# Seven block products for the second half of w_ff2, and S5's input shuffled in whole rows

## The chip, the core and the metric

One core of a Trainium2 chip runs the whole program. Its engines work side by side, each through its own list in order: TensorE (PE, matmuls; its weight loads are shown as PEld), VectorE (DVE), ScalarE (ACT), GpSimd (POOL) and SyncE (SP, which only issues transfers here). The metric is device time in microseconds (us), lower is better.

## The reference

One layer of a decoder trunk on 1024 tokens of width 1024. What the change touches is the feed-forward network at its end and the input of one of three mixers, S5:

```python
proj = h @ w_in[l]
aq, ak, av, su, cq, ck, cv, cg = jnp.split(proj, offsets, axis=-1)
o_b = s5_mixer(su, ...)     # 16 groups x 16 channels, 64 complex states a group
...
x = x + ga1 * (mix @ w_out[l])
h = rms_norm(x, norm2_g[l]) * (1 + sc2) + sh2
x = x + ga2 * (jnp.square(jax.nn.relu(h @ w_ff1[l])) @ w_ff2[l])
```

w_ff1 is 1024 x 4096, w_ff2 4096 x 1024. `ga2` is one row of 1024 gates, the same for all tokens.

## The kernel before

Every float32 product is made of three matmuls (`mm3`, line 369): each operand is split into a high part (an ACT copy that rounds) and a low part (a difference on DVE or POOL), and high x high, high x low and low x high are added up in PSUM. So a weight page of 128 x 1024 costs one load, one ACT copy and one difference before PE can use it.

The feed-forward network runs in two halves of 512 tokens. The hidden width is cut into 32 blocks of 128 (`NF`). `ff1` makes one block for 512 tokens: 8 x 3 matmuls of 512 columns into one PSUM bank, then relu, square and the split (`ff_act`). `ff2` takes two blocks and one half of the output width: for each of four tiles of 128 tokens 2 x 3 matmuls of 512 columns, which DVE adds into the accumulator `z[n]`. After the last pair DVE multiplies `z[n]` by the gates (`rows_of[5]`), adds the residual `x2[n]`, and SP stores the tile. The second half begins when all tokens are normed (`N2 7`), some 1080 us into the program, and nothing but the feed-forward network is left then. `load_ff` loads a weight page, copies the high part on ACT and takes the low part on POOL.

S5 (`s5`, line 1003) gets its input `su` in four PSUM banks, channel by partition. ACT and DVE copy them into two pages `ut`, by position within a chunk of eight tokens; SP writes these to a scratch tensor in HBM, `su_d`, and reads them back with another layout into two pages `Ur`. `build` makes S5's weights, splits them and splits `Ur` (tiles named k); `apply` multiplies.

The order is not that of the code: all calls are recorded with a rank, a list scheduler (`arrange`, line 173) plays them through with its own prices, and the program is issued in the order that comes out. It also hands out the SBUF pages: 38 pages of 1024 floats per partition (`b`), 10 of 804 (`u`), 4 of 1088 (`k`) and a few others (`SLOTS`). All issued instructions therefore carry one line, that of the replay (2002 before, 2201 after). PSUM has eight banks, printed pa0 to pa3 (`sg`) and pb0 to pb3 (`sh`).

Of the kernel before, what the change touches and what calls it, by code (L numbers as in the profile page):

```python
# [9 lines left out]
F32 = mybir.dt.float32  # L10
# [3 lines left out]
ALU = mybir.AluOpType  # L14
# [6 lines left out]
NT = 8  # L21
# [289 lines left out]
def trunk(ctx: ExitStack, tc: tile.TileContext, I, out):  # L311
# [686 lines left out]
                tt(r, r, dd[:, g2 * 8 + hf * 4:g2 * 8 + hf * 4 + 4], ALU.add)  # L998
        yield 0

    su_d = dr.tile([2, 2, 65536], F32, name="su_d")

    def s5():

        for g2 in range(2):
            ut = page(1024)
            utv = ut.rearrange("f (j c) -> f j c", j=8)
            for q in range(2):
                src = sh[g2 * 2 + q].rearrange("f (c j) -> f j c", j=8)
                d = utv[:, :, q * 64:q * 64 + 64]  # L1010
                if q == 0:
                    A.activation(out=d, in_=src, func=AF.Copy)
                else:
                    V.tensor_copy(out=d, in_=src)
            nc.sync.dma_start(out=su_d[:, g2].rearrange("hf (q c) -> hf q c", q=64), in_=ut)
        done.add("s5 taken")
        Ur = [page(1024) for _ in range(2)]
        for hf in range(2):
            for j in range(8):
                nc.sync.dma_start(  # L1020
                    out=Ur[hf][j * 16:j * 16 + 16].rearrange("p (g c) -> p g c", g=8),
                    in_=su_d[hf].rearrange("g2 (g p j c) -> j p (g2 g) c", g=4, p=16, j=8)[j])
        W, Us = [], []
        Y = [page(1024) for _ in range(2)]
        Sj = [page(1024) for _ in range(2)]
# [884 lines left out]
        spawn(T + 9, late_proj())  # L1910


    z, f_of, w_of = {}, {}, {}
    pace, ahead = [X_FF], [X_AHEAD]

    def load_ff(unit):
# [29 lines left out]
    def ff2(half, p, dh, b):  # L1946
# [3 lines left out]
            load_row(5)  # L1950
        for t in range(4):
            n = half * 4 + t
            if n not in z:
                z[n] = page(1024)
            if last and not dh:
                x2[n] = page(1024)
                nc.sync.dma_start(out=x2[n], in_=x2_d[n])
            o, s, d = take("f2"), t * 128, z[n][:, c]
            for e in range(2):
                f = f_of[half, p * 2 + e]  # L1960
                w = slice(e * 512, e * 512 + 512)
                mm3(o, f[:, s:s + 128], f[:, 512 + s:640 + s], b[0][:, w], b[1][:, w], e == 0, e == 1)
            if p == 0:
                V.tensor_copy(out=d, in_=o)
            else:
                tt(d, o, d, ALU.add)
            if last:
                tt(d, d, rows_of[5][:, c], ALU.mult)
                tt(d, d, x2[n][:, c], ALU.add)
                if dh:  # L1970
                    nc.sync.dma_start(out=out[n * 128:n * 128 + 128, :], in_=z[n])
            yield 1.28 * pace[0]

    def feed_forward():
        units, h = [], NF // 2
        for q in range(NF + 1):
            for e in range(2):
                if q < NF:
                    units.append((1, q // h, q % h * 2 + e, 0))
                if q:  # L1980
                    units.append((2, (q - 1) // h, (q - 1) % h, e))
        loaded = 0
        for j, u in enumerate(units):
# [2 lines left out]
                loaded += 1  # L1986
            kind, half, i, dh = u
            if kind == 1:
                if half:
                    while f"N2 {NT - 1}" not in done:  # L1990
                        yield 1.0
                    pace[0] = 1.0
                yield from ff1(half, i, w_of.pop(u))
            else:
                yield from ff2(half, i, dh, w_of.pop(u))

    run_plan()
    order, span, start, end = arrange(calls, tag_of, SLOTS)
# [8 lines left out]
def pack(inputs):  # L2007
# [21 lines left out]
    wog = lambda a: a.reshape(2, 3, 64, 1024).transpose(1, 0, 2, 3).reshape(3, 128, 1024)  # L2029
    wi = I["w_in"][0]  # L2030
    span = lambda *ab: np.concatenate([np.arange(a, b) for a, b in ab])
    cols = [span((640, 896)), span((0, 384)), span((384, 640)), span((896, 1280), (2048, 2066)),
            span((1280, 1408), (1664, 1792)), span((1408, 1664)), span((1792, 2048))]
    group = lambda a: a.reshape(4, 2, 128, -1).transpose(0, 2, 1, 3).reshape(-1)
    return dict(
# [29 lines left out]
```

## Time and profile before

| | |
|---|---|
| three runs | 1436.9, 1441.61 (median), 1446.45 us |
| profiled execution | 1440.49 us, its span 1438.8 us |
| busy, share of the span | PE 93%, DVE 57%, ACT 53%, POOL 53% |
| granted TensorE clock, mean | 0.965 of 2.4 GHz |
| matmuls | 7218 recorded |
| DMA | 160.5 MB, 112 GB/s in the mean |

The page gives sums over one execution. A tile's name is that of the program without its number. "Idle before" is the time for which an engine stood still ahead of an instruction, and the name behind the arrow is what ended it. A timeline merges instructions of one kind that follow each other, and shows those waits in brackets. The chain of waits is followed back from the last instruction to what released it.

### The profile page before, as it was taken

To read this page: it belongs to the slowest core of one execution; us is meant where nothing else is said; L and a number is where in the kernel's file an instruction comes from. 1 tells how busy PE (TensorE), PEld (TensorE's weight loads), DVE (VectorE), ACT (ScalarE), POOL (GpSimd) and SP (SyncE) were. 2 spreads that over 40 slices of the span, in tenths; PEclk is the share of its full clock that TensorE was granted. 3 is DMA by queue.
4 is the path that set the end of the run, shared out by engine and by line. 5 is a ranking of instruction groups with operands and counts; after the bars stand their busy time and mean duration, and the time that the engine had idled before them with its cause. 6 is when DMAs were issued, how large, how long until landed. Compare 5 with 4: busy or idle time off the path is not lost.

```text
span 1438.8 us, 20631 instructions
## 1 busy us (share of the span) xinstructions
PE 1343.4 (93%) x7218; PEld 1154.1 (80%) x7218; DVE 813.2 (57%) x1846; ACT 760.8 (53%) x1774; POOL 759.8 (53%) x700
## 2 busy tenths in 40 slices
PE   5796799899899868999999999999999999999997
PEld 4696799899798646888888888888888888888886
DVE  7863777688688764556466565464538222222225
ACT  5265548667779766655565565552263333233331
POOL 2654683512556544546555555675557655554650
PEclk9888999999999887999999999999999999999999
DMA  9415334531315231222222222233444332233231
GB/s 357 141 51 163 128 101 159 176 100 58 111 42 177 90 123 46 94 67 70 74 79 87 79 96 74 79 127 138 160 176 175 104 108 97 89 104 101 88 118 58
DMA packets 58185, 160.54 MB, mean 112 GB/s; under 512 B 6468, under 2 KB 22370, under 8 KB 58082
## 3 DMA queue, kind: packets, MB, share of 16 engines
q1 hardware_dynamic: 50273, 145.33, 30.3%
q10 hardware_dynamic: 7808, 13.91, 2.6%
q8 instruction: 56, 0.92, 0.3%
q14 instruction: 48, 0.39, 0.1%
HBM read 140.07 MB, written 19.14 MB: 111 GB/s over the span
## 4 chain that ended last, share of the span: by engine, by line
PE 77%; DVE 6%; ACT 5%; DMA 1%; issue 1%; POOL 0%; ACTq 0%; SPq 0%; POOLq 0%; DVEq 0%
PE pb L2002 43%; PE pa L2002 33%; DVE b L2002 3%; ACT b L2002 3%; ACT u L2002 1%; DVE pb L2002 1%; DMA cq_d<-s 1%; DVE u L2002 1%; DVE k L2002 0%; DMA b<-in_ada_dram 0%; DVE s L2002 0%; DVE small L2002 0%; ACT s L2002 0%; POOL s L2002 0%; ACT k L2002 0%
## 5 line engine op out<-in xcount | busy, mean ns | idle before, releaser
L2002 PE MATMUL pb<-b,b 128*128 128x512 f32 (+2 forms) x2646 | 634.4, 386 | 3.6 <-DVE b L2002 2.4
L2002 PEld LDWEIGHTS pb<-b,b 128*128 128x128 f32 (+1 forms) x2646 | 478.4, 190 | 93.7 <-DVE b L2002 3.1
L2002 POOL TENSOR_TENSOR b<-b,b 128x1024 fp32r<-128x1024 f32 (+6 forms) x172 | 388.9, 2274 | 107.5 <-ACT b L2002 83.2
L2002 PE MATMUL pa<-b,b 128*128 128x256 f32 (+3 forms) x1890 | 352.4, 334 | 11.1 <-ACT s L2002 6.7
L2002 PEld LDWEIGHTS pa<-b,b 128*128 128x128 f32 (+1 forms) x1890 | 286.4, 195 | 41.0 <-ACT s L2002 7.0
L2002 DVE TENSOR_TENSOR b<-pa,b 128x512 f32<-128x512 f32 (+3 forms) x158 | 98.3, 622 | 245.7 <-PE pa L2002 242.8
L2002 ACT ACTIVATE b<-b 128x1024 fp32r<-128x1024 f32 (+2 forms) x195 | 187.9, 983 | 66.9 <-DVE b L2002 39.8
L2002 PE MATMUL pa<-u,b 128*128 128x384 f32 (+2 forms) x836 | 206.5, 366 | 5.6 <-ACT u L2002 2.6
L2002 POOL TENSOR_TENSOR b<-r,b 128x512 fp32r<-128x512 f32 x65 | 85.6, 1316 | 174.5 <-ACT b L2002 174.4
L2002 ACT ACTIVATE r<-pb 128x512 f32<-128x512 f32 x64 | 38.2, 597 | 244.8 <-PE pb L2002 244.8
L2002 PEld LDWEIGHTS pa<-u,b 128*128 128x128 f32 x836 | 147.8, 206 | 16.3 <-ACT u L2002 7.7
L2002 ACT ACTIVATE u<-pa 128x384 fp32r<-128x384 f32 (+4 forms) x205 | 97.1, 479 | 93.4 <-PE pa L2002 90.9
L2002 DVE TENSOR_TENSOR b<-pb,b 128x512 f32<-128x512 f32 (+2 forms) x150 | 98.1, 657 | 71.2 <-PE pb L2002 66.9
L2002 DVE TENSOR_TENSOR u<-pa,u 128x384 fp32r<-128x384 f32 (+1 forms) x173 | 95.0, 553 | 63.3 <-ACT u L2002 60.0
L2002 POOL TENSOR_SCALAR u<-u,small 128x256 f32<-128x256 f32 (+3 forms) x90 | 52.7, 596 | 115.8 <-DVE small L2002 77.7
L2002 POOL TENSOR_SCALAR b<-b,small 128x64 f32<-128x64 f32 (+8 forms) x118 | 78.2, 672 | 59.9 <-DVE small L2002 50.6
L2002 PE MATMUL pa<-wide,b 128*128 128x128 f32 (+1 forms) x443 | 83.9, 301 | 16.2 <-DVE b L2002 10.3
L2002 ACT ACTIVATE b<-b,small 128x128 f32<-128x128 f32 x256 | 93.3, 524 | 5.5 <-DMA b<-in_ada_dram 3.3
L2002 PEld LDWEIGHTS pa<-wide,b 128*128 128x128 f32 (+1 forms) x443 | 58.8, 151 | 35.1 <-DVE b L2002 13.0
L2002 DVE TENSOR_TENSOR b<-b,b 128x512 f32<-128x512 f32 (+3 forms) x78 | 78.2, 1028 | 11.1 <-ACT b L2002 5.3
L2002 PE MATMUL pb<-k,u 128*128 128x320 f32 (+10 forms) x300 | 71.3, 344 | 10.1 <-ACT u L2002 6.2
L2002 ACT ACTIVATE b<-pb,small 128x64 f32<-128x64 f32 (+4 forms) x130 | 62.5, 494 | 28.8 <-DVE small L2002 25.7
(148 smaller groups left out, 1492.6 us busy)
## 6 DMA issues: line engine op xcount, KB each, us to landing
b<-in_ff_dram SPq DMA_DIRECT2D x128, 512.0 KB, 3.8
b<-in_ada_dram SPq DMA_DIRECT2D x48, 512.0 KB, 4.6
b<-in_x_dram SPq DMA_DIRECT2D x16, 512.0 KB, 9.5
b<-in_wo_dram SPq DMA_DIRECT2D x16, 512.0 KB, 4.5
r<-in_w_in_dram SPq DMA_DIRECT2D x16, 256.0 KB, 2.8
b<-in_cw_dram SPq DMA_DIRECT2D x8, 512.0 KB, 5.0
x_d<-b ACTq DMA_DIRECT2D x8, 512.0 KB, 3.4
b<-x_d SPq DMA_DIRECT2D x8, 512.0 KB, 5.6
```

Source lines behind the costliest of these rows:

```text
L2002: method(*args, **kw)
```

## The change

**S5's input.** The scratch tensor gets the shape [2, 8, 128, 128]. A page `ut` is written with its 128 partitions outermost, each in eight runs of 128 floats, instead of two halves of 64 rows of 1024 floats. `Ur` is read in four transfers of 128 rows of 512 floats instead of sixteen of 16 x 8 x 128. The columns of `w_in` for `su` are put in another order on the host, so that position and channel stand where whole rows need them.

On SP, where the stored input of S5 leaves and comes back (b_196 and b_197 are the pages `ut`, b_198 and b_199 the pages `Ur`), before:

```order
L2002 DMA b138_219<-in_ada_dram 128x1024
L2002 DMA su_d_98<-b115_196 2x64x1024
L2002 DMA su_d_98<-b116_197 2x64x1024
L2002 DMA b117_198<-su_d_98 16x8x128 x8
L2002 DMA b118_199<-su_d_98 16x8x128 x8
L2002 DMA b147_228<-in_ada_dram 128x1024
```

and now:

```order
L2201 DMA b138_219<-in_ada_dram 128x1024
L2201 DMA su_d_98<-b115_196 128x8x128
L2201 DMA su_d_98<-b116_197 128x8x128
L2201 DMA b117_198<-su_d_98 128x512
L2201 DMA b118_199<-su_d_98 128x512
L2201 DMA b117_198<-su_d_98 128x512
L2201 DMA b118_199<-su_d_98 128x512
L2201 DMA b147_228<-in_ada_dram 128x1024
```

The place in the queue is the same; the shapes changed, and sixteen reads became four, of which the first two read what the first write stored.

On ACT, at the same stage (k127 and k143 are the high parts of the two pages `Ur`, b123 and b124 S5's weights out of PSUM, b146 belongs to the conditioning, s129 and u130 to a projection), before:

```order
L2002 ACTIVATE b146_227<-b138_219,small_71 128x128 x2
L2002 ACTIVATE s129_210<-pa1_64 128x384
L2002 ACTIVATE u130_211<-pa1_64 128x384
L2002 ACTIVATE b123_204<-pb1_68 128x4x64
L2002 ACTIVATE b124_205<-pb1_68 128x4x64
L2002 ACTIVATE k127_208<-b117_198 128x1024
L2002 ACTIVATE b146_227<-b138_219,small_71 128x128 x4
L2002 ACTIVATE k143_224<-b118_199 128x1024
```

and now:

```order
L2201 ACTIVATE b137_218<-b114_195,small_71 128x128 x5
L2201 ACTIVATE k127_208<-b117_198 128x1024
L2201 ACTIVATE k143_224<-b118_199 128x1024
L2201 ACTIVATE b123_204<-pb1_68 128x4x64
L2201 ACTIVATE b124_205<-pb1_68 128x4x64
L2201 ACTIVATE b123_204<-pb3_70 128x4x64
L2201 ACTIVATE b124_205<-pb3_70 128x4x64
L2201 ACTIVATE b123_204<-pb0_67 128x4x64
L2201 ACTIVATE b124_205<-pb0_67 128x4x64
L2201 ACTIVATE b146_227<-b138_219,small_71 128x128 x2
L2201 ACTIVATE s129_210<-pa1_64 128x384
L2201 ACTIVATE u130_211<-pa1_64 128x384
```

Both copies of `Ur` moved ahead of all eight evacuations of the weights (the last two follow these rows) and of two of the projection's.

**Second half of w_ff2.** Of its 16 pairs of hidden blocks the first 14 are taken in seven groups of four blocks (`NG` = 7). A group is a product of 512 tokens x 512 hidden x 1024 outputs, cut in two along each side, so of eight block products; it is now made of seven, with sums of blocks formed beforehand and afterwards (Strassen's scheme in Winograd's form). Sums of weight blocks (`right`) and of activation blocks (`left_rest`) are formed on DVE, split into high and low, and each product (two tiles of 128 tokens, 2 x 3 matmuls of 512 columns each) is added by DVE into one or two of six accumulators. The last group's four blocks are multiplied as before (`last_ff2`), with the gates multiplied into its weights (`load_last`); the seven groups' accumulators get their sums, the gates and the residual in `finish_block`, so that `last_ff2` adds and stores, half a tile at a time.

```diff
-    su_d = dr.tile([2, 2, 65536], F32, name="su_d")
+    su_d = dr.tile([2, 8, 128, 128], F32, name="su_d")
...
-            nc.sync.dma_start(out=su_d[:, g2].rearrange("hf (q c) -> hf q c", q=64), in_=ut)
+            nc.sync.dma_start(out=su_d[g2].rearrange("j f c -> f j c"), in_=utv)
...
-            for j in range(8):
-                nc.sync.dma_start(
-                    out=Ur[hf][j * 16:j * 16 + 16].rearrange("p (g c) -> p g c", g=8),
-                    in_=su_d[hf].rearrange("g2 (g p j c) -> j p (g2 g) c", g=4, p=16, j=8)[j])
+            for g2 in range(2):
+                src = su_d[g2].rearrange("j (p hf g) c -> hf (j p) (g c)", p=16, hf=2)[hf]
+                nc.sync.dma_start(out=Ur[hf][:, g2 * 512:g2 * 512 + 512], in_=src)
...
-                if dh:
-                    nc.sync.dma_start(out=out[n * 128:n * 128 + 128, :], in_=z[n])
+                nc.sync.dma_start(out=out[n * 128:n * 128 + 128, c], in_=d)
...
+    PRODUCTS = {1: ("X", ("C11", "U")), 2: ("Y", ("C11",)), 6: ("Z", ("U",)), 7: ("X", ("P7",)), 5: ("Y", ("P5",)),
+                4: ("Z", ("P4",)), 3: ("X", ("P3",))}
...
+    def split_right(g, m, x):
+        hi, lo = page(1024), page(1024)
+        copy_hi(hi, x)
+        split_lo(V, lo, x, hi)
+        right_of[g, m] = hi, lo
+    def right(g, m):
+        B = wraw[g]
+        if m == 1:
+            B["T1"] = page(1024)
+            tt(B["T1"], B[0, 1], B[0, 0], ALU.subtract)
+        elif m == 2:
+            B["T2"], B["T4"] = page(1024), page(1024)
+            tt(B["T2"], B[1, 1], B["T1"], ALU.subtract)
+            tt(B["T4"], B[1, 0], B["T2"], ALU.subtract)
+        elif m == 6:
+            tt(B[0, 1], B[1, 1], B[0, 1], ALU.subtract)
+        split_right(g, m, B[{1: (0, 0), 2: (1, 0), 6: "T2", 7: (0, 1), 5: "T1", 4: "T4", 3: (1, 1)}[m]])
...
+    def split_left(g, m, src):
+        left_of[g, m] = u = page(1024)
+        two = lambda x: x.rearrange("p (e t) -> p e t", e=2)
+        copy_hi(two(u[:, 0:512]), src)
+        split_lo(V, two(u[:, 512:1024]), src, two(u[:, 0:512]))
...
+        split_left(g, 2, a(0, 1))
+        s1 = of(a(1, 0), a(1, 1), ALU.add)
+        s2 = of(s1, a(0, 0), ALU.subtract)
+        split_left(g, 6, s2)
+        yield
+        split_left(g, 7, of(a(0, 0), a(1, 0), ALU.subtract))
+        split_left(g, 5, s1)
+        yield
+        split_left(g, 4, a(1, 1))
+        split_left(g, 3, of(a(0, 1), s2, ALU.subtract))
...
+    def product(g, m):
+        bank_, to = PRODUCTS[m]
+        b, u = right_of.pop((g, m)), left_of.pop((g, m))
+        for s in range(2):
+            o = dict(X=sg[2:4], Y=sg[0:2], Z=sh[2:4])[bank_][s]
+            for e in range(2):
+                l = e * 256 + s * 128
+                w = slice(e * 512, e * 512 + 512)
+                mm3(o, u[:, l:l + 128], u[:, 512 + l:640 + l], b[0][:, w], b[1][:, w], e == 0, e == 1)
+            for name in to:
...
+                    tt(d, o, d, ALU.add)
...
+    def finish_block(m, dh, d):
+        if d == "P5":
+            acc["U5"] = page(1024)
+            tt(acc["U5"], acc["U"], acc["P5"], ALU.add)
+            tt(acc[d], acc["U5"], acc["P7"], ALU.add)
+        else:
+            for x in {"P4": ("P7", "U"), "P3": ("U5",)}.get(d, ()):
+                tt(acc[d], acc[d], acc[x], ALU.add)
+        for s in range(2):
+            n, c = 4 + m * 2 + s, slice(dh * 512, dh * 512 + 512)
+            z_at[n, dh] = o = acc[d][:, s * 512:s * 512 + 512]
+            tt(o, o, rows_of[5][:, c], ALU.mult)
+            tt(o, o, x2[n][:, c], ALU.add)
...
+        tt(two(raw), two(raw), row.to_broadcast([128, 2, 512]), ALU.mult)
...
+    def last_ff2():
...
+                tt(d, o, d, ALU.add)
+                nc.sync.dma_start(out=out[(4 + t) * 128:(5 + t) * 128, c], in_=d)
...
+        for g in range(NG):
+            after = [[("p", g, m) for m in ms] for ms in ((1, 2), (6, 7), (5, 4), (3,))]
+            for e in range(4):
+                f = [("f", g * 4 + 4 + e)]
+                items += after[e] + f if g == NG - 1 and e == 3 else f + after[e]
```

The last lines set the order: a block of w_ff1 for the next group, then products 1 and 2; a block, 6 and 7; a block, 5 and 4; a block, 3.

On DVE, in the middle of the second half, before (accumulators b1292 to b1295, banks pa and pb):

```order
L2002 TENSOR_TENSOR b1292_1373<-pa3_66,b1292_1373 128x512
L2002 TENSOR_TENSOR b1293_1374<-pb2_69,b1293_1374 128x512
L2002 TENSOR_TENSOR b1294_1375<-pb3_70,b1294_1375 128x512
L2002 TENSOR_TENSOR b1295_1376<-pa2_65,b1295_1376 128x512
L2002 TENSOR_TENSOR b1292_1373<-pa3_66,b1292_1373 128x512
```

and now, around product 3 of a group (b1365 is accumulator P3, b1414 and b1430 the next group's activations, u1446, u1447 and u1453 sums of their blocks, b1445, b1448, b1451 to b1454 left blocks; b1319 and b1320 are the accumulators C11 and U of product 1):

```order
L2201 TENSOR_TENSOR b1365_1446<-pa2_65,b1365_1446 128x512
L2201 TENSOR_TENSOR u1446_1527<-b1414_1495,b1430_1511 128x512
L2201 TENSOR_TENSOR b1445_1526<-b1430_1511,b1445_1526 128x512
L2201 TENSOR_TENSOR u1447_1528<-u1446_1527,b1414_1495 128x512
L2201 TENSOR_TENSOR b1451_1532<-u1446_1527,b1451_1532 128x512
L2201 TENSOR_TENSOR b1452_1533<-b1430_1511,b1452_1533 128x512
L2201 TENSOR_TENSOR b1448_1529<-u1447_1528,b1448_1529 128x512
L2201 TENSOR_TENSOR u1453_1534<-b1430_1511,u1447_1528 128x512
L2201 TENSOR_TENSOR b1365_1446<-pa3_66,b1365_1446 128x512
L2201 TENSOR_TENSOR b1454_1535<-u1453_1534,b1454_1535 128x512
L2201 TENSOR_TENSOR b1319_1400<-pa2_65,b1319_1400 128x512
L2201 TENSOR_TENSOR b1320_1401<-pa2_65,b1320_1401 128x512
```

Before, DVE had only one addition per PSUM bank in this half; now seven operations between SBUF tiles stand between the two evacuations of one product, and an eighth ahead of product 1's.

## Rows read from the trace of the kernel before

**Rows 1.** The page: busy us of the engines; the chain by engine.

```profile
PE 1343.4 (93%) x7218; PEld 1154.1 (80%) x7218; DVE 813.2 (57%) x1846; ACT 760.8 (53%) x1774; POOL 759.8 (53%) x700
...
PE 77%; DVE 6%; ACT 5%; DMA 1%; issue 1%; POOL 0%; ACTq 0%; SPq 0%; POOLq 0%; DVEq 0%
```

**Rows 2.** Busy time of each engine (and instructions) in stretches of 100 us.

```profile
core 0: us, PE busy (x) PEld busy (x) DVE busy (x) ACT busy (x) POOL busy (x), PEclk, DMA share, GB/s
...
100.00:200.00 100.00, 76.44 (x506) 74.11 (x506) 56.97 (x91) 52.88 (x141) 59.47 (x50) 0.89 0.43 133
...
1100.00:1200.00 100.00, 100.00 (x443) 82.82 (x442) 29.67 (x43) 37.10 (x50) 58.83 (x30) 1.00 0.41 142
1200.00:1300.00 100.00, 100.00 (x443) 82.84 (x442) 26.13 (x38) 33.81 (x45) 58.31 (x29) 1.00 0.30 98
1300.00:1400.00 100.00, 100.00 (x443) 82.84 (x442) 25.03 (x37) 33.84 (x45) 54.13 (x27) 1.00 0.32 106
```

**Rows 3.** The chain of waits near the end: start, us, what.

```profile
1408.21 5.44 PE pb L2002 x24
```

**Rows 4.** Timeline of SP's queue: start us, us, what.

```profile
91.18 1.22 SPq L2002 DMA_DIRECT2D su_d<-b  x2
114.26 7.72 SPq L2002 DMA_DIRECT2D b<-su_d  x16
```

**Rows 5.** Waits of SP's queue: in total, times, longest.

```profile
SPq L2002 <- DMA su_d<-b: 21.7, 1, 21.7
```

**Rows 6.** Timeline of all engines: start us, us, what [idle before].

```profile
105.31 0.67 ACT L2002 ACTIVATE b<-pb 128x256 fp32r<-128x256 f32 x2
...
120.72 1.06 ACT L2002 ACTIVATE k<-b 128x1024 fp32r<-128x1024 f32 x1 [14.74 <-DMA b<-su_d]
...
121.80 1.23 DVE L2002 TENSOR_TENSOR k<-b,k 128x1024 fp32r<-128x1024 f32 x1 [15.04 <-ACT k L2002]
...
121.83 0.79 PE L2002 MATMUL pb<-b,k 128*128 128x256 f32 x2 [14.31 <-ACT k L2002]
```

**Rows 7.** Two short stretches, columns as in group 2.

```profile
100.00:105.00 5.00, 5.00 (x31) 4.93 (x31) 2.27 (x7) 3.64 (x12) 0.00 (x0) 0.81 0.13 52
...
115.00:117.00 2.00, 0.00 (x0) 0.00 (x0) 0.00 (x0) 0.00 (x0) 0.00 (x0) 0.50 0.42 124
```

**Rows 8.** DMA queues, and issues with size and median us to landing.

```profile
q10 hardware_dynamic: 7808, 13.91, 2.6%
...
b<-in_ff_dram SPq DMA_DIRECT2D x128, 512.0 KB, 3.8
...
r<-in_w_in_dram SPq DMA_DIRECT2D x16, 256.0 KB, 2.8
...
out_dram<-b SPq DMA_DIRECT2D x8, 512.0 KB, 3.2
```

**Rows 9.** Groups by shape, 1060 to 1430 us: busy us, mean ns.

```profile
L2002 POOL TENSOR_TENSOR b<-b,b 128x1024 fp32r<-128x1024 f32 x67 | 161.7, 2438 | 12.4 <-ACT b L2002 12.4
...
L2002 ACT ACTIVATE b<-b 128x1024 fp32r<-128x1024 f32 x63 | 63.0, 1044 | 8.6 <-DMA b<-in_ff_dram 8.6
...
L2002 DVE TENSOR_TENSOR b<-b,b 128x512 f32<-128x512 f32 x26 | 26.9, 1078 | 0.1
L2002 ACT ACTIVATE r<-r 128x512 f32<-128x512 f32 x33 | 20.9, 632 | 1.0
```

**Rows 10.** Timeline: DVE near 129 us, PE and DVE at the end.

```profile
128.82 1.22 DVE L2002 TENSOR_TENSOR k<-b,k 128x1024 fp32r<-128x1024 f32 x1
129.95 1.21 DVE L2002 TENSOR_REDUCE s<-b 128x128 f32<-128x1024 f32 x1
...
1428.45 1.52 PE L2002 MATMUL pa<-b,b 128*128 128x512 f32 x6
...
1432.67 0.68 DVE L2002 TENSOR_TENSOR b<-pa,b 128x512 f32<-128x512 f32 x1
1433.27 2.01 DVE L2002 TENSOR_TENSOR b<-b,b 128x512 f32<-128x512 f32 x3
```

## What the change will do to the time: the prediction

> **What bounds the kernel now.** I read the page first: TensorE (PE) is busy for 93% of the span and holds 77% of the chain that ended last [rows 1]. Then the table by stretches of 100 us: the share is not even. From 1100 to 1400 us PE is busy for every microsecond at full clock, while DVE, ACT and POOL stand at a quarter, a third and a half; between 100 and 200 us it is busy for only three quarters [rows 2]. So there are two different places. In the second half of the feed-forward network matmuls are the bound: only fewer of them shorten it. The chain prints 24 of them in 5.44 us, back to back [rows 3], 0.2267 us each. In the early place something else is waited for.
>
> The timelines around 91 to 122 us show what. SP issues the two writes of S5's input at 91.18 and then nothing until 114.26; of this, 21.7 us are put down to the landing of those writes [rows 4, 5]. Behind it PE idles 14.3, ACT 14.7 and DVE 15.0 us, all three ending with the copy of the shuffled input at 120.72 [rows 6]: the whole core stands still. In the middle of the write the DMA share is 0.13, two of sixteen engines, at 52 GB/s [rows 7]; two is also the outermost dimension of the write.
>
> **S5's shuffle.** Removed: the 2x64x1024 writes and sixteen reads of 64 KB, issued over 7.72 us [rows 4]. Added: two writes whose outermost dimension is 128 partitions, in 512 B runs (1024 per write), and four reads of 256 KB in 2 KB runs. No row shows this write. Its bounds: reads in 512 B runs moved 124 GB/s at a share of 0.42 [rows 7], so 0.42 x 16 x 2 us = 13.4 engine-us for 248 KB or 484 runs, 28 ns a run; ACT's queue, mostly writes, spent 2.6% of 16 x 1438.8 us on 7808 packets [rows 8], 77 ns a packet of 1.8 KB. So 1024 runs over 16 engines take 1.8 to 4.9 us of transfer. A plain 512 KB store lands in 3.2 us [rows 8]. With the issues done at 92.4 (91.18 + 1.22), both writes have landed between 96.5 and 104; I take 98, near the read's price, since the runs have that size. If instead a run costs what a 4 KB row costs now (52 GB/s over two engines: 158 ns), the two writes take 2048 x 158 / 16 = 20 us and nothing is gained; that is the far bound.
>
> A 256 KB load lands in 2.8 us [rows 8]; of the four reads two need only the first write, so I count 4.5 us: the input is there at 102.5 (101 to 110). The order of ACT changes with it: both copies of the input (1.06 us each) now stand ahead of the evacuations of S5's weights, which ACT did until 105.98, before the stall [rows 6]. These now queue behind the wait, and PE, which applies the weights, waits for them: eight pieces at 0.33, about 2 us of other small activations and two hops, some 5 us. So PE applies S5's weights at 102.5 + 1.06 + 5 = 108.6 instead of 121.83: 13.3 us earlier. PE's idle time caps this at 14.3; input at 110 would leave 5.7. I take **13 us**. Whether it lasts to the end cannot be read from a row: every queue behind it moves up together, SP's loads included (SP is free 20 us sooner), but the scheduler has also put rows of every engine in another order up to about 250 us. I give this 4 us either way and nothing to the sum.
>
> **Second half, matmuls.** Before, a pair of hidden blocks took 2 x 24 matmuls for w_ff1 and 2 x 24 for w_ff2. Now seven groups of four blocks need 96 for w_ff1 and seven products of 12 = 84 instead of 96 for w_ff2; the last group keeps 96. Removed: 7 x 12 = 84 matmuls of the same 512 columns, 84 x 0.2267 = **19.0 us**. A group's period is 180 x 0.2267 = 40.8 us instead of 43.5.
>
> **What has to hide under it.** Per group, counted from the order. POOL: four differences of 128x1024 at 2.44 us [rows 9], 9.8 us (before: eight, and four narrow ones). ACT: eleven copies at 1.04, seven narrow ones and eight of relu and square at about 0.63: 20.9 us, 51% of the period. DVE: sixteen additions or copies out of PSUM, eleven operations of 128x1024 and eleven of 128x512 between SBUF tiles. Start to start these take 0.60, 1.13 and 0.66 us where nothing disturbs them [rows 10]: 9.6 + 12.4 + 7.3 = 29.3 us, 72%, up from a quarter. So no engine passes PE in the mean, and this costs nothing as long as DVE isn't disturbed.
>
> It is disturbed where POOL reads SBUF as well: 26 DVE operations of 128x512 at the start of this half, beside POOL's, took 1.08 us in the mean [rows 9] against 0.67 alone (three in 2.01) [rows 10]. The page "SBUF — State Buffer" of the Trainium skill (section "SBUF: two separate sides") says that a GpSimd operation and a DVE operation with two SBUF inputs lock each other out for a whole instruction. By that rule POOL's 9.8 us could all be added to DVE: 39.1 of 40.8 us; the slower mean in the row agrees in direction. In the mean DVE stays under PE, so what decides is a burst.
>
> The tightest burst stands in the order of DVE: between the two evacuations of product 3 (banks pa2 and pa3) stand seven narrow operations for the next group's left blocks. The first evacuation can start 1.36 us before product 3 ends on PE; 0.60 + 7 x 0.66 = 5.2 us later comes the second, done 4.5 us after the end of product 3. Bank pa3 is wanted by product 1 of the next group after one block of w_ff1 and half a product: 5.44 + 1.36 = 6.8 us. Slack 2.3 us. One POOL operation of 2.44 us in between uses it up; a second one stalls PE by 2.4. Lowest price 0, highest 7 x 2.4 = 17 us; I take **1 us** in all, since POOL is busy for only a quarter of the period.
>
> The other covers: group 0's first product stands behind five blocks of w_ff1 (27 us of PE) that need only the normed input; the last block's activation, about 4 us, lies beside final matmuls of the three earlier blocks. The block additions after product 3 (some 11 us of DVE) lie under 72 matmuls, 16.3 us, before a bank is wanted again. If those covers failed, each would cost its own length once.
>
> **The end.** Now the last matmul ends at 1429.97, DVE works off its gate and residual additions until 1435.28, the store lands 3.2 us later, and the span ends at 1438.8 [rows 8, 10]: 8.8 us after PE. Afterwards gate and residual are already in the weights and accumulators: one addition of 0.68, a store of half the size (no more than 3.2) and the same 0.3: 4.2 us. Saves **4.5 us**.
>
> **Sum.** The profiled execution took 1440.49 us (span 1438.8). 1440.5 - 13 - 19.0 - 4.5 + 1 = 1405.0. The median of the three runs shown lies 1.1 us above the profiled one, so I forecast 1406.
>
> **Rivals.**
> A: the shuffle gives nothing. For it: the far bound above, and ACT now waits earlier in its order, with work behind it that it used to do meanwhile. Against: only two engines moved the write. Time: 1406 + 13 = 1419.
> B: DVE bursts stall PE by up to 2.4 us a group. For it: the stretched rows and 2.3 us of slack. Against: means of 72% and a POOL at a quarter. Time: 1406 + 16 = 1422.
> C, on the other side: SBUF. There are 38 pages of 4 KB per partition; counting what a group keeps (8 of normed input, 6 accumulators, 4 of activations, 7 left blocks, 4 raw weights, 3 sums, 4 raw of the next group, 6 of right parts, 6 for w_ff1) gives 48, so some cannot overlap. If a right block is loaded late, PE waits for one load, copy and split: 3.8 + 1.04 + 1.23 = 6.1 us a group [rows 8 to 10], 43 us in all; against 36.5 us of gains this gives 1448, and half-rate matmuls after a pause (clock 0.50 at 115 to 117 [rows 7]) could add to it. It decides from 36.5 / 7 = 5.2 us a group on. Against: ACT waited only 8.6 us in all for 63 weight copies [rows 9], so loads run ahead.
> D: the other order up to 250 us gives back the S5 gain in other waits; same time as A, and counted with it.
>
> **How the numbers follow.** Forecast 0.74 (its own range 1397 to 1413: the 4 us of the other order, 13 us of shuffle within its bounds), A and D 0.12, B 0.11, C 0.03. The range that holds 8 in 10 runs from 1398 to 1421: it leaves out the outer ends of the forecast, most of B's far end and C. About 1%, 14.4 us, is what a measurement of this kernel can tell from no change. The forecast and A are faster by more (under 1427.2), so is nearly all of B; C falls half on either side of 1456. So faster 0.95, within 0.03, slower 0.02.
>
> **What would show it.** Matmul records in the second half 84 fewer, PE at 100% in its stretches, 24 still in 5.44 us; DVE near 70 to 80%; no idle of PE over 2 us put down to su_d; DMA share well above 0.13 while the input is written; the span ending about 4 us after the last matmul. I am wrong if PE shows gaps put down to DVE or to weight loads in each period of 41 us, or if S5's products start after 115 us.

## The result and the profile after

The changed kernel takes 1406.03 us (median of 4 runs, 1404.26 to 1406.35) where the kernel before took 1441.69 on the same chip: ratio 0.975, 95% interval 0.9717 to 0.9783. The profiled execution took 1406.35 us with a span of 1404.6, 34.2 us less than that of before. Measured twice more later, the ratio was 0.9721 (0.9705 to 0.9738) and 0.9711 (0.9688 to 0.9734), 1403.28 and 1403.27 us. The forecast was 1406.0.

The page after, busy us and the chain by engine, to be held against [rows 1]:

```profile
PE 1330.2 (95%) x7134; PEld 1142.1 (81%) x7134; DVE 973.0 (69%) x2005; ACT 796.8 (57%) x1816; POOL 652.9 (46%) x640
...
PE 72%; DVE 5%; ACT 4%; issue 1%; DMA 0%; POOL 0%; ACTq 0%
```

84 matmuls are gone (7218 to 7134), DVE has 160 us more, POOL 107 less. By stretches, against [rows 2]:

```profile
core 0: us, PE busy (x) PEld busy (x) DVE busy (x) ACT busy (x) POOL busy (x), PEclk, DMA share, GB/s
100.00:200.00 100.00, 90.62 (x592) 87.30 (x591) 65.08 (x107) 58.78 (x156) 68.70 (x63) 0.91 0.41 131
1100.00:1200.00 100.00, 100.00 (x443) 82.84 (x442) 79.52 (x94) 48.67 (x62) 28.92 (x11) 1.00 0.35 120
1200.00:1300.00 100.00, 100.00 (x443) 82.84 (x442) 81.91 (x98) 49.53 (x65) 21.06 (x8) 1.00 0.32 106
1300.00:1400.00 100.00, 98.28 (x433) 80.78 (x432) 82.61 (x95) 38.24 (x49) 27.40 (x11) 1.00 0.23 77
```

PE has gained 14.2 busy us between 100 and 200 us. In the middle of the second half it is busy throughout, with DVE at 80% beside it. Only the last row is not full.

**S5's shuffle.** SP's queue, its wait for the writes, and the DMA share while they run (columns as above), against [rows 4, 5, 7]:

```profile
91.94 1.01 SPq L2201 DMA_DIRECT2D su_d<-b  x2
96.96 2.13 SPq L2201 DMA_DIRECT2D b<-su_d  x4
```

```profile
SPq L2201 <- DMA su_d<-b: 4.5, 2, 4.0
```

```profile
92.00:94.00 2.00, 2.00 (x32) 1.75 (x31) 0.46 (x1) 1.45 (x5) 2.00 (x8) 1.00 0.57 156
94.00:96.00 2.00, 2.00 (x40) 2.00 (x38) 0.00 (x0) 0.00 (x0) 1.92 (x8) 1.00 1.07 284
```

The wait falls from 21.7 to 4.5 us and the share rises from 0.13 to about 1. Behind it, against [rows 6]:

```profile
102.24 2.00 ACT L2201 ACTIVATE k<-b 128x1024 fp32r<-128x1024 f32 x2 [8.79 <-DMA b<-su_d]
...
109.23 0.52 PE L2201 MATMUL pb<-b,k 128*128 128x256 f32 x3
```

PE applies S5's weights without a wait at this place, 12.6 us earlier than before (121.83).

**The second half.** A mark that both traces have are the last four transposes ahead of it (pa<-wide,b, 128x128): at 1047.86 before, at 1033.36 after, 14.5 us earlier. From there to the end of the last matmul it takes 382.11 us before (1429.97) and 367.09 after (1400.45): 15.0 less, not 19.0. In before no wait of PE stands in that stretch. After has these, in total and in place:

```profile
PE pa L2201 <- DVE b L2201: 1.9, 2, 1.4
PE pb L2201 <- DVE b L2201: 1.3, 1, 1.3
```

```profile
1067.38 1.65 PE L2201 MATMUL pa<-b,b 128*128 128x512 f32 x6 [1.41 <-DVE b L2201]
...
1374.70 0.73 PE L2201 MATMUL pb<-b,b 128*128 128x512 f32 x2 [1.26 <-DVE b L2201]
1375.90 0.73 PE L2201 MATMUL pa<-b,b 128*128 128x512 f32 x2 [0.46 <-DVE b L2201]
```

One is at the end of the first half and two are in the last group; in the 300 us between them there is none. The chain shows PE at its old pace there, and the end:

```profile
1316.55 5.44 PE pb L2201 x24
...
1400.48 0.69 DVE b L2201
```

From the last matmul to the end of the span it is now 1404.6 - 1400.45 = 4.15 us, where it was 8.83: one addition and a half-size store. So the 34.2 us of the spans are 14.5 + 15.0 + 4.7.

### The profile page after: what moved, and what is told of

It reads as the page before. It is cut to its first block, busy times and chain, and to the rows that moved or that the text cites. A ratio compares the mean times of both kernels' runs of the same rounds, so it can differ in the third digit from the quotient of the medians.

```text
span 1404.6 us, 20524 instructions
## 1 busy us (share of the span) xinstructions
PE 1330.2 (95%) x7134; PEld 1142.1 (81%) x7134; DVE 973.0 (69%) x2005; ACT 796.8 (57%) x1816; POOL 652.9 (46%) x640
## 4 chain that ended last, share of the span: by engine, by line
PE 72%; DVE 5%; ACT 4%; issue 1%; DMA 0%; POOL 0%; ACTq 0%
PE pb L2201 41%; PE pa L2201 31%; ACT b L2201 3%; DVE b L2201 2%; ACT u L2201 1%; DVE pb L2201 1%; DVE k L2201 0%; DVE u L2201 0%; DMA cq_d<-s 0%; DVE small L2201 0%; DVE s L2201 0%; ACT s L2201 0%; ACT k L2201 0%; POOL s L2201 0%; ACTq L2201 0%
## 5 line engine op out<-in xcount | busy, mean ns | idle before, releaser
L2201 PE MATMUL pb<-b,b 128*128 128x512 f32 (+2 forms) x2478 | 591.9, 386 | 3.7 <-DVE b L2201 3.7
L2201 PEld LDWEIGHTS pb<-b,b 128*128 128x128 f32 (+1 forms) x2478 | 446.9, 190 | 87.3 <-DVE b L2201 5.1
L2201 POOL TENSOR_TENSOR b<-b,b 128x1024 fp32r<-128x1024 f32 (+6 forms) x140 | 317.7, 2276 | 319.2 <-ACT b L2201 211.5
L2201 PE MATMUL pa<-b,b 128*128 128x256 f32 (+2 forms) x1974 | 367.3, 336 | 10.8 <-DVE b L2201 6.0
L2201 PEld LDWEIGHTS pa<-b,b 128*128 128x128 f32 (+1 forms) x1974 | 302.4, 195 | 44.5 <-DVE b L2201 8.0
L2201 ACT ACTIVATE b<-b 128x1024 fp32r<-128x1024 f32 (+5 forms) x265 | 241.1, 926 | 114.1 <-DVE b L2201 44.4
L2201 DVE TENSOR_TENSOR b<-b,b 128x1024 fp32r<-128x1024 f32 (+4 forms) x181 | 203.2, 1153 | 18.2 <-ACT b L2201 11.2
L2201 DVE TENSOR_TENSOR b<-pa,b 128x512 f32<-128x512 f32 (+3 forms) x176 | 108.6, 626 | 69.7 <-PE pa L2201 66.1
L2201 DVE TENSOR_TENSOR b<-pb,b 128x512 f32<-128x512 f32 (+2 forms) x120 | 76.0, 647 | 53.0 <-PE pb L2201 51.0
L2201 PE MATMUL pa<-wide,b 128*128 128x128 f32 (+1 forms) x443 | 84.4, 303 | 14.5 <-DVE b L2201 10.2
L2201 POOL TENSOR_TENSOR b<-r,b 128x512 fp32r<-128x512 f32 x37 | 52.3, 1412 | 54.8 <-ACT b L2201 54.6
L2201 ACT ACTIVATE u<-pb,small 128x256 f32<-128x256 f32 (+6 forms) x126 | 59.7, 484 | 28.3 <-DVE small L2201 26.4
```

The source lines that it names most:

```text
L2201: method(*args, **kw)
```

## The experiments

All ratios are to the kernel before on the same chip. "Stretch" means the time from the last transposes to the end of the last matmul, read from each trace; it is 382.11 us before and 367.1 in the changed kernel.

### The two parts apart

**The feed-forward part alone** (the changed kernel with S5's shuffle of before):

```
-            nc.sync.dma_start(out=su_d[g2].rearrange("j f c -> f j c"), in_=utv)
+            nc.sync.dma_start(out=su_d[:, g2].rearrange("hf (q c) -> hf q c", q=64), in_=ut)
...
-            for g2 in range(2):
+            for j in range(8):
```

> The kernel after with S5's scratch tensor, write, reads and column order as before; only the second half of w_ff2 is new. Theory: the two parts lie in stages that don't overlap, so their gains add up; between the two profiled executions marks before the second half moved up by 14.5 us, and from there on the new kernel is 19.7 us shorter (15.0 us on PE, 4.7 us after it). Expected 1406 + 14.5 = 1420.5 us, 1418 to 1423. Rival (the gains overlap, or the other order up to 250 us carries part of the 14.5 us): another time, below 1417 or above 1424. The stall of 14 us at S5's input is there again.

Measured: 1425.54 us, ratio 0.9865 (0.9847 to 0.9883), 19.5 us less. As a time this is above the expected 1418 to 1423, since the kernel before took 1445.5 us beside it; as a gain it is the 19.7 us that were expected. Its stretch is 367.09 us and its waits are those of the changed kernel, to the tenth. S5's products start at 121.73.

**S5's shuffle alone** (the kernel before with the new writes, reads and column order), measured twice:

```
-            nc.sync.dma_start(out=su_d[:, g2].rearrange("hf (q c) -> hf q c", q=64), in_=ut)
+            nc.sync.dma_start(out=su_d[g2].rearrange("j f c -> f j c"), in_=utv)
```

> The kernel before with the new scratch tensor, write, four reads and column order; the feed-forward network is the old one. Theory: 1441.7 - 14.5 = 1427.2 us, 1425 to 1430. Rival: S5's gain lasts only because the second half is new: above 1432.

> The kernel before with the change of S5's input shuffle alone, a second time and in more rounds, to size that step; nothing else is edited. Theory 1 (the step is worth what PE's first use of S5's weights shows in the profiles, 121.8 to 108.5 us, as the prediction had it): 13 to 14.5 us, ratio 0.990 to 0.991. Theory 2 (it is worth more, since the 14 us of PE's wait are followed by some 14 us at half clock in which PE has work, and both get shorter; in the profiles so far the last transposes come 15 to 22 us earlier): 18 to 22 us, ratio 0.985 to 0.988.

Measured: 1420.98 us, 0.9845 (0.9806 to 0.9885), and 1425.3, 0.9869 (0.9847 to 0.9891). That is 22.4 and 18.9 us, not 13. The first run missed both of its expectations; the second met the number of theory 2, but half clock, the reason given there, turns out to be the smaller part (see "S5, the size" below).

**The writes alone.** The kernel before, with each page written by two transfers of 64 partitions; the sixteen reads of before stay.

```
-            nc.sync.dma_start(out=su_d[:, g2].rearrange("hf (q c) -> hf q c", q=64), in_=ut)
+            for hf in range(2):
+                nc.sync.dma_start(out=su_d[hf, g2].rearrange("(q c) -> q c", q=64), in_=ut[hf * 64:hf * 64 + 64])
```

> The kernel before with one edit: each page is stored to the old place by two writes of 64 rows of 1024 floats, instead of one of 2x64x1024; same bytes, same runs of 4 KB, the sixteen short reads stay. Theory: the stall came from the write's outermost dimension of two, which kept it on two engines; now the writes land some 4 to 5 us after their issue, the reads take 7.7 us to issue and 3 to land, so that the input is there at about 107 instead of 124: PE applies S5's weights about 13 us earlier, 1429 us (1426 to 1433). Rival: the short reads and their issues are the cost: at most 3 us are gained, 1439 us or more.

Measured: 1422.31 us, 0.9849 (0.983 to 0.9868). Its SP queue, and the share while it writes:

```profile
90.81 3.10 SPq L2003 DMA_DIRECT2D su_d<-b  x4
96.93 7.72 SPq L2003 DMA_DIRECT2D b<-su_d  x16
```

```profile
92.00:94.00 2.00, 2.00 (x41) 2.00 (x39) 0.00 (x0) 0.32 (x2) 1.92 (x8) 1.00 1.01 229
```

The same bytes in the same rows of 4 KB, with 64 instead of 2 outermost, are read back from 96.93 on, as early as in the changed kernel, and the gain is that of the whole new shuffle, 19 to 25 us by the interval, where 13 were expected. So the wait went because the write used more engines; the whole rows and the four reads bring nothing that can be measured. That all of the gain comes from the engines isn't shown, though, because this edit too made the scheduler put out another order. PE's matmuls pa<-b,b of one projection, before the next pa<-ones,s, in the kernel before, with S5's shuffle alone and with the writes alone:

```profile
172.31 8.44 PE L2002 MATMUL pa<-b,b 128*128 128x256 f32 x51 [3.38 <-ACT s L2002]
```

```profile
154.56 11.36 PE L2001 MATMUL pa<-b,b 128*128 128x256 f32 x74 [1.63 <-ACT s L2001]
```

```profile
152.95 11.05 PE L2003 MATMUL pa<-b,b 128*128 128x256 f32 x74 [1.19 <-ACT s L2003]
```

No run has the spread write in the old order. The page "DMA: Bandwidth & Descriptors" of the Trainium skill (section "Why a DMA increments its semaphore by 16 and not by 1") says that a transfer runs on the largest number of engines, up to 16, that divides the slowest dimension of both sides. The shares agree: 0.13 with 2 outermost [rows 7], 1.01 with 64, 1.07 with 128.

**Do the parts add?** The changed kernel again, beside the experiments that follow:

> The changed kernel itself once more, on the same chip as the three that follow, so that these can be compared with it and with the kernel before at once; nothing is edited. Theory 1 (the two parts of the change do not quite add: both are followed by the same later stretch, and a little of what each gains alone is the same microseconds): ratio 0.975 to the kernel before, 36 us below it. Theory 2 (they add, and the difference between 36 us and the 19.5 and 22.4 us measured apart is the spread of the kernel before, whose runs lie up to 9 us apart): 0.9865 x 0.9845 = 0.971, 42 us below it.

> The changed kernel again on the same chip as the other three of this call, for their comparison; nothing is edited. 0.972 to 0.975 of the kernel before, and 367.1 us from the last transposes to the last matmul, with 3.1 us of waits of PE in them.

Measured: 0.9721 and 0.9711, 39.5 and 40.7 us. The product of the parts is 0.971 with the first measurement of S5's shuffle alone and 0.974 with the second: they add, within the intervals, as theory 2 had it. The stretch was 367.11 us in the first and 368.69 in the second, where PE's clock fell right behind the waits in the last group (PEclk 0.51 from 1373 to 1376), so the expected 367.1 was missed there by 1.6 us.

### Where the four microseconds of the second half went

**The blocks' sums moved.** In the last group the sums, gates and residuals of P4 are placed after product 3, and those of P5 and P3 between the last eight tiles:

```
-                if it[1] == NG - 1 and it[2] in BLOCKS:
-                    finish_block(*BLOCKS[it[2]])
+                if it[1] == NG - 1 and it[2] in (2, 3):
+                    for _ in finish_block(*BLOCKS[{2: 2, 3: 4}[it[2]]]):
...
+                for _ in range(2):
+                    next(rest, None)
```

> The changed kernel, with the page additions, gates and residuals of the finished blocks in another place: those of P4 after product 3 of the last group, those of P5 and P3 two at a time after the bank additions of the last eight tiles. No operation is added or removed. Theory (the failed term of the prediction is this: the additions of the finished blocks stand in VectorE's queue ahead of bank additions for which PE waits, 1.26 + 0.46 us at 1374.70 and 1375.90 and a restart of the pipeline of 0.16 each): -2.0 us against the changed kernel, no PE wait behind 1360 us. Rival (VectorE is simply full there, and the same operations hold up the last tiles instead): 0 to +2 us, with the waits of PE between 1380 and 1400 us.

Measured: 1404.81 us, 0.9731 (0.9715 to 0.9747), stretch 367.29 us. The two waits became one of the same place and nearly the same size:

```profile
1367.19 4.55 DVE L2214 TENSOR_TENSOR b<-b,b 128x1024 f32<-128x1024 f32 x2
1368.25 2.41 POOL L2214 TENSOR_TENSOR b<-b,b 128x1024 fp32r<-128x1024 f32 x1 [1.00 <-ACT b L2214]
...
1373.59 0.74 PE L2214 MATMUL pa<-b,b 128*128 128x512 f32 x2 [2.00 <-DVE b L2214]
```

Both theories missed: no gain, and no wait among the last tiles either. In the changed kernel DVE's rows at this place are:

```profile
1368.36 5.69 DVE L2201 TENSOR_TENSOR b<-b,b 128x1024 f32<-128x1024 f32 x3
...
1373.97 0.68 DVE L2201 TENSOR_TENSOR b<-pb,b 128x512 f32<-128x512 f32 x1
```

The last of them is the late addition out of a bank. By the order of issue the three ahead of it are the sum U + P5, the low part of a page of the last weights and the sum for P5; P5's sums stand behind product 5 in this kernel, not behind product 3. The edit took only the third away: the scheduler put U + P5 in the same place again. So this run doesn't clear the sums. Its two operations take 4.55 us beside POOL, 2.3 each instead of 1.22.

**The gate back at the end:**

```
-        tt(two(raw), two(raw), row.to_broadcast([128, 2, 512]), ALU.mult)
...
                 tt(d, o, d, ALU.add)
+                tt(d, d, rows_of[5][:, c], ALU.mult)
+                tt(d, d, x2[4 + t][:, c], ALU.add)
```

> The changed kernel with the gate and the residual taken back to the very end: the last group's weights are loaded without the gate, the finished blocks are not gated, and each of the last eight tiles gets bank addition, gate and residual after its own twelve matmuls. Everything is still computed. Theory (what shortened the end by 4.7 us is that each half row is written as soon as it is finished, not where the gate stands): behind the last matmul stand two more operations of 128x512, 2 x 0.64 = 1.3 us, while the 1.7 us of PE idle around 1375 us go with the 16 gate and residual operations that are in VectorE's queue there: 0 to -1 us against the changed kernel on this chip. Rival (the gate in the weights is what brought the 4.5 us of the end): +4.5 us.

Measured: 1403.18 us, 0.9722 (0.9704 to 0.974), the same as the changed kernel beside it (0.9721). In the trace the waits in the last group are gone and the stretch is 364.89 us, 2.2 less; from the last matmul to the end it takes 5.3 us instead of 4.15. So the theory holds in the main: of the 4.7 us at the end, 3.5 (8.83 to 5.3) stay without the gate in the weights and come from adding and storing each half tile as soon as its matmuls are done. The early gate is worth the other 1.2 us, and costs 2.2 ahead of it.

**All low parts of the second half on DVE:**

```
-        split_lo(G, lo, raw, hi)
+        split_lo(low, lo, raw, hi)
...
-        load_ff((1, 1, i, 0))
+        load_ff((1, 1, i, 0), V)
```

> The changed kernel with the low parts of the second half's w_ff1 on VectorE too, so that POOL has almost only the activation's multiplication left there. VectorE then has 4 x 1.22 = 4.9 us more per group, by undisturbed durations 29.3 + 4.9 = 34.2 of 40.8 us (84%). Theory (what costs VectorE is POOL working beside it: the same operation of 128x512 takes 0.6 to 0.7 us alone and 2.3 us beside POOL's 2.8 us): its busy time per 100 us in the steady state grows by less than the 12 us that the count gives, PE stays at 100% there, and the time is that of the changed kernel, -1 to +2 us. Rival (VectorE's number of operations is the bound): above 90% busy in the middle, PE waits of 1 us and more per group, +10 us.

Measured: 1403.64 us, 0.9728 (0.9712 to 0.9744). DVE's groups by shape from 1100 to 1375 us, first of the changed kernel on the same chip, then with POOL idle (busy us, mean ns | idle before):

```profile
L2201 DVE TENSOR_TENSOR b<-b,b 128x1024 fp32r<-128x1024 f32 x49 | 68.9, 1418 | 2.4 <-POOL b L2201 2.4
L2201 DVE TENSOR_TENSOR b<-pa,b 128x512 f32<-128x512 f32 x74 | 49.0, 685 | 16.1 <-PE pa L2201 15.4
...
L2201 DVE TENSOR_TENSOR u<-b 128x512 f32<-128x512 f32 x6 | 15.7, 2615 | 0.0
```

```profile
L2201 DVE TENSOR_TENSOR b<-b,b 128x1024 fp32r<-128x1024 f32 x75 | 90.0, 1219 | 17.1 <-PE pb L2201 10.5 <-ACT b L2201 3.2 <-issue 3.1
L2201 DVE TENSOR_TENSOR b<-pa,b 128x512 f32<-128x512 f32 x71 | 46.7, 684 | 12.4 <-PE pa L2201 12.3
...
L2201 DVE TENSOR_TENSOR u<-b 128x512 f32<-128x512 f32 x6 | 4.1, 683 | 0.0
```

The operation on one page (u<-b, one per group, in the same place each time) falls from 2615 to 683 ns, the wide ones from 1418 to 1219, and those that read PSUM do not move. So DVE takes over 26 wide operations and is busy for only 79.3 and 83.9 us in the two full stretches, where it was 78.2 and 81.4: as the theory has it. In the prediction the page "SBUF — State Buffer" of the Trainium skill (section "SBUF: two separate sides") stood for adding POOL's time to DVE's. Its list of those locked out (DVE with two SBUF inputs against POOL reading SBUF) fits these rows, since u<-b takes both its inputs from one SBUF page. The sum does not fit: u<-b and the wide ones lose 11.6 and 9.8 us of the 68.2 that POOL's wide operations take.

At the end of the first half this kernel loses more than it wins (its stretch is 370.22 us, 3.1 more than the changed kernel's): DVE's splits of the first weights queue behind its gates and residuals, and PE waits 4.86 us, then runs at half clock:

```profile
1065.86 19.46 PE L2201 MATMUL pb<-b,b 128*128 128x512 f32 x76 [4.86 <-DVE b L2201]
```

```profile
1061.00:1066.00 5.00, 0.14 (x1) 0.14 (x1) 5.00 (x9) 1.33 (x2) 0.00 (x0) 0.72 0.88 276
1066.00:1070.00 4.00, 4.00 (x10) 3.17 (x11) 4.00 (x5) 1.62 (x2) 0.00 (x0) 0.50 0.87 269
1070.00:1074.00 4.00, 4.00 (x19) 3.29 (x18) 4.00 (x4) 0.86 (x2) 0.00 (x0) 1.00 1.01 408
```

**The order at the end of the first half.** The second half's first w_ff1 block stands again between the two sides of the first half's last w_ff2 unit:

```
+                if i == h - 1 and dh:
...
+                    yield from late_ff1(0, w_of.pop((1, 1, 0, 0)))
                 yield from ff2(half, i, dh, w_of.pop(u))
```

> The changed kernel with the order of the kernel before at the end of the first half: the second half's first w_ff1 block (24 matmuls, 5.44 us) stands between the two sides of the first half's last w_ff2 unit again, not behind both. No operation is added or removed. Theory (the wait of 1.42 us there comes from eight tiles of six matmuls, 1.36 us each, standing back to back, while VectorE has an addition, a gate and a residual for each, 0.69 + 1.28 = 1.97 us, so that it falls behind by 0.6 us a tile; in the kernel before the block stood between them and no wait is there): the wait of PE behind the first half goes, -1.6 us from the last transposes to the last matmul, which is 367.1 us in the changed kernel. Rival (what holds VectorE up there is POOL splitting the first two late weights beside it, two operations of 128x512 in 3.5 us): the wait stays or moves into the block, 0 us.

Measured: 1400.37 us, 0.9692 (0.967 to 0.9713), stretch 365.37, 1.7 less than 367.1. Its only waits in the second half are the two of the last group:

```profile
PE pb L2203 <- DVE b L2203: 1.3, 1, 1.3
PE pa L2203 <- DVE b L2203: 0.5, 1, 0.5
```

So the first wait came from the change of order, eight tiles of 1.36 us back to back against 1.97 us of DVE for each.

**That order, and DVE for the splits from the fifth block on** (`load_ff((1, 1, i, 0), G if i < 4 else V)` beside the edit above):

> The same as the run with the order at the end of the first half, and the low parts of the second half's w_ff1 on VectorE from its fifth block on, so that POOL is idle beside VectorE in the steady state and in the last group, and the first four blocks' splits are off VectorE's queue at the edge. Theory: the 1.25 + 0.46 us in the last group go as well (there VectorE's operations of 128x1024 were stretched from 1.22 to 1.9 us by POOL), without the 4.86 us that VectorE's splits cost at the edge with all blocks on VectorE: from the last transposes to the last matmul 367.1 - 1.6 - 2.0 = 363.5 us, which is what the 84 matmuls alone leave of 382.1 (363.1). In time -3.5 us against the changed kernel, 1399.5 us. Rival (VectorE's added operations come back as waits in groups 0 and 1): 366 us and more.

Measured: 1399.71 us, 0.9692 (0.9673 to 0.9712). No wait of PE is left. The marks of its stretch, in the timeline and in the chain:

```profile
1028.36 0.60 PE L2203 MATMUL pa<-wide,b 128*128 128x128 f32 x4
```

```profile
1388.72 2.73 PE pa L2203 x12
```

1391.45 - 1028.36 = 363.09 us: 19.0 less than before, exactly what 84 matmuls cost. In time both versions lie below the changed kernel (2.9 and 3.6 us by the medians of that chip), but the intervals overlap; what is shown is the stretch.

**The right blocks' low parts on POOL** (`split_lo(G, lo, x, hi)` in `split_right`):

> The changed kernel with the low parts of the seven right blocks of each group on POOL and not on VectorE: 7 x 2.4 = 17 us more of POOL per group of 40.8 us, 8.5 us less of VectorE. Theory (VectorE and POOL stretch each other's operations; what one gains by the other's taking an operation it loses while that runs beside it): the mean of VectorE's operations goes up, those of 128x512 on one page from 2.6 us and those of 128x1024 from 1.4 us, VectorE is not below 75% busy, and POOL's operations of 128x1024 take over 2.5 us; right blocks come later, and waits of PE on them begin, +3 to +15 us. Rival (no such coupling, VectorE is the engine that needs relief): VectorE falls to 60%, the waits at both edges go, -2 us.

Measured: 1406.44 us, 0.9736 (0.9711 to 0.9761), stretch 373.25. DVE and POOL from 1100 to 1375 us:

```profile
L2201 DVE TENSOR_TENSOR b<-b,b 128x1024 f32<-128x1024 f32 x30 | 60.4, 2046 | 3.0 <-POOL b L2201 2.6 <-PE pa L2201 0.3
...
L2201 DVE TENSOR_TENSOR u<-b 128x512 f32<-128x512 f32 x6 | 10.0, 1661 | 0.0
```

```profile
L2201 POOL TENSOR_TENSOR b<-b,b 128x1024 fp32r<-128x1024 f32 x71 | 181.3, 2573 | 84.0 <-ACT b L2201 37.4 <-PE pa L2201 32.8 <-PE pb L2201 11.1
```

DVE's wide sums go from 1.22 to 2.05 us, as expected; the one on one page does not go up but down, since POOL's operations now fall on others. DVE is 65 to 69% busy, so neither number held. PE stays full from 1100 to 1300 us all the same, and loses 5.13 us at one place, in the last group, with half clock behind it. The time is 3.2 us above the changed kernel beside it (1403.27), inside what the theory gave, though the intervals overlap.

## Why the prediction was right, and where it was not

**The two places** were the right ones. PE's wait for S5 is gone, and matmuls bound the second half: with the last waits taken away it is shorter by 19.0 us, the term as written.

**S5, the times: right.** Forecast, with the measured time behind it: writes landed 98 (reads start 96.96), input there 102.5 (102.24), weights applied 108.6 (109.23), each within 1.1 us. So of the bounds the price per run taken from a read was the near one.

**S5, the size: mis-sized.** "13 us" was the earlier start of PE and no more, and "PE's idle time caps this at 14.3" was wrong. In the first pair of traces 13 fits (14.5 at the last transposes). Against the time it does not: S5's shuffle alone brought 18.9 and 22.4 us, the writes alone 21.8; 0.9847 to 0.9868 (19 to 22 us) lies in all three intervals. What failed is the term for the other order of issue up to about 250 us, to which the prediction gave "4 us either way and nothing to the sum". A mark that all fourteen traces have are four transposes behind a wait for DVE's k, before and after:

```profile
351.55 0.66 PE L2002 MATMUL pa<-wide,b 128*128 128x128 f32 x4 [0.69 <-DVE k L2002]
```

```profile
335.37 0.66 PE L2201 MATMUL pa<-wide,b 128*128 128x128 f32 x4 [0.69 <-DVE k L2201]
```

The two kernels with the old shuffle reach it at 351.55 and 353.43 us, the twelve with the new shuffle or writes between 329.43 and 336.19, 20.4 us earlier in the mean. At the first S5 product it is 13.8 us and at the last transposes 20.2, so the gain is complete at the mark. Between the first S5 product and the mark, before and after, columns as above:

```profile
121.83:351.55 229.72, 213.40 (x1526) 207.39 (x1526) 170.71 (x337) 153.67 (x412) 112.59 (x123) 0.95 0.41 132
```

```profile
109.23:335.37 226.14, 213.56 (x1529) 207.17 (x1528) 167.66 (x335) 151.76 (x409) 116.97 (x132) 0.95 0.40 129
```

PE stands still there for 15.1 and 16.3 us with the old shuffle and for 9.2 to 12.6 with the new one, 5.2 less in the mean: shorter waits in another order. The rest, 1.4 us in the mean, is shorter busy time of PE, and what half clock (1.2 of 2.4 GHz) cost more before can only lie in this part: from 120 to 130 us PE worked at a mean clock of 0.71 then, and after it has 1.00 from 110 to 120.

```profile
120.00:130.00 10.00, 8.18 (x45) 7.88 (x45) 4.32 (x9) 6.00 (x14) 1.01 (x1) 0.71 0.69 167
```

```profile
110.00:120.00 10.00, 9.89 (x71) 9.47 (x70) 6.14 (x16) 6.95 (x22) 9.35 (x15) 1.00 0.55 166
```

Whether the new order or the earlier input shortened the waits, no run separates; that stays open. That the first pair showed only 14.5 us is the spread of single executions: the one that the sum was built on was a good one. Its mean clock was 0.965, while the 32 runs of the same kernel beside the experiments show 0.951 to 0.962, and medians of 1442.8 to 1445.5 us. The feed-forward part alone, with the same S5, reached the last transposes at 1053.20, not 1047.86; the changed kernel's first profile, at 1033.36, is the latest of the twelve (1026.12 to 1033.36). So 13 us stand in the sum where the typical run loses about 20.

**The burst: right.** PE has no wait on DVE in the steady state, with DVE at 80%. DVE's operations were stretched as feared (one in each group takes 2.6 us), and the 2.3 us of slack held.

**The covers: the failed step of the second half.** "The block additions after product 3 lie under 72 matmuls before a bank is wanted again" (shortened) put all of them behind product 3 and counted only them. P5's two sums stand behind product 5, with the low part of a page of the last weights between them; the three took 5.69 us beside POOL, and DVE came 1.26 and then 0.46 us late to the banks. Without POOL's splits beside it (both runs with the splits on DVE) the wait is gone, and also without the early gate's operations (the weights' multiplications and the blocks' gates and residuals together), while the sums stayed in all of these runs. So the sums alone don't make DVE late; which of the operations ahead counts most isn't separated. And one cover was never listed: before, a w_ff1 block stood between the two sides of the first half's last unit; moving the second half into its own loop took it away (1.41 us). These make 3.1 of the 4.0 us by which the stretch is longer than the removed matmuls leave (367.09 against 382.11 - 19.04), where the sum has 1; the other 0.9 goes too when the waits go (363.09).

**The end** was forecast at 4.5 and is 4.7 us. The reason was only partly right: 3.5 us come from the half tiles, 1.2 from the gate in the weights.

**Rivals.** A and D fell with the shuffle's own runs. B's mechanism is there (DVE's operations are stretched beside POOL), but its price was not paid. C did not come: nothing in the second half waits for a load.

**The sum.** 1406 was met to 0.1 us in the first measurement, with 36 us gained; the two later ones gave 40 us, and the intervals overlap. The steps made 35.5 with two errors of opposite sign: the shuffle some 7 us too low, the second half with its end 3 too high (22.5 against 19.5 measured alone). That the number was met so much more closely than its terms is luck.

## What to carry to other kernels

Before costing what a moved transfer is worth, look at its outermost dimension: with an edit of two lines that makes it 64 instead of 2, and the order of issue that came with it, this kernel gained as much as with the whole new shuffle, about 20 us. When work is put into a loop of its own, list what stood between its neighbours before and is now gone, and count the whole queue of the engine that has to hand back a bank, in the order of issue, not just the operations that were added. Where a list scheduler sets the order, compare the orders before and after every edit: a change of one transfer can move what stands around it. Where one profile carries the sum, compare its mean granted clock with the other runs first.

## What was not expected of the hardware

DVE operations of 128x512 that read PSUM took 684 to 685 ns whether POOL was busy or idle, while one from SBUF alone went from 683 to 2615 ns. A wait of PE of 4.86 us was followed by some 4 us at half clock; the waits of 1.26 and 0.46 us in the last group were followed by half clock in one run (PEclk 0.51 from 1373 to 1376) and by full clock in another (1.00).
